# Order of the recurrence branch's output projection: four contraction steps of its second output tile stand ahead of the first tile's last two, and the second tile's weights are split sooner

## The chip, the cores and the metric

One NeuronCore of a Trainium2 chip runs the whole program. The metric is the device time of one execution in microseconds (us); lower is better. Five engines work side by side and meet only at semaphores: PE (TensorE, matrix products; PEld is its weight load), DVE (VectorE), ACT (ScalarE), POOL (GpSimd) and SP (SyncE, which here does nothing but issue transfers, one after another).

## The reference, cut to what matters

The program is a two-layer backbone over 1024 latent tokens and 256 context tokens, 1024 channels wide. The change lies in the first layer, whose output is the sum of two branches behind one projection:

```python
def even_mixer(h, h0, p):
    z = h @ p["w_in"]
    va, vg, ga, xb, gb = jnp.split(z, ...)
    y_a = conformer_conv(va, vg, p) * jax.nn.silu(ga)
    y_b, hT = rglru_branch(xb, p, h0, True)
    y_b = y_b * jax.nn.silu(gb)
    return jnp.concatenate([y_a, y_b], axis=-1) @ p["w_out"], hT
...
x = x + gate[:, None] * out_x
```

The recurrence branch is `y_b`. Its half of the last product, `y_b @ w_out[1024:]`, is 1024 tokens by 1024 channels, contracted over 1024 channels. This product is what the change reorders.

## The kernel before, in words

Everything lies transposed: 128 channels on the partitions, tokens along the free axis, in two halves of 512 (`HALF[0]`, `HALF[1]`). 1024 channels are `KT` = 8 tiles. A product in full precision is made of three rounded ones: a tile is split into a high part (a cast on ACT) and a low part (a subtraction of the cast from the tile), and `hi*hi + hi*lo + lo*hi` is added up in PSUM. So one *contraction step* (one of the eight channel tiles, one half of the tokens) is three matmuls of 128x128 by 128x512, and one output tile of 128 channels is 8 steps x 2 halves x 3 = 48 matmuls.

The part in question comes when the recurrence has ended. The scan's results lie in DRAM (`yb_raw[n]`). For each channel tile n, `gated(n, ...)` (L1040) makes the operand of the projection: per half it loads `yr` (L1044, into one of the two buffers of `vpool`), multiplies it with the gate `sb` (DVE), casts it to `ybh` (ACT), and subtracts to get `ybl` (DVE). Between these, `fill(k)` (L642) puts k pieces of the convolution branch on DVE, which have nothing to do with the projection but have to be done at some time.

While DVE makes those operands, PE computes the gate products `gb4` to `gb7` (48 matmuls each, `gb_product`, L841). Then it goes over to the projection tiles, which the trace calls `wob` (8 output tiles m, two halves each: `wob0_0`, `wob0_1`, `wob1_0` and so on).

Weights come through `gb_weights(j)` (L835): a load into one of two raw buffers (`wr`), a cast into one of two high buffers (`wh`, ACT) and a subtraction into one of two low buffers (`wl`, POOL). Index 4 to 7 is `gb`, 8 to 15 is `wob0` to `wob7`, 16 and 17 are two tiles of the next gate. With two buffers, the raw load of weight j + 2 has to wait for the split of weight j, and the split of j + 2 for the last matmul that uses j.

All of this is issued through `on(engine, ...)` (L497), which chains each instruction behind the one issued before on its engine: the order on PE, ACT, DVE and POOL is the order of the code. Only SP's transfers are placed by the scheduler. Almost all of these instructions are recorded under line L501, so the profile is read by tile names.

The code around the change, with its line numbers:

```python
513    def mm3_fixed(ps, w, xs, cols):
...
516        for k in range(KT):
517            kc = slice(k * P, (k + 1) * P)
518            on("pe", nc.tensor.matmul, ps, hi[:, kc], xh[k][:, cols], start=(k == 0), stop=False)
519            on("pe", nc.tensor.matmul, ps, hi[:, kc], xl[k][:, cols], start=False, stop=False)
520            on("pe", nc.tensor.matmul, ps, lo[:, kc], xh[k][:, cols], start=False, stop=(k == KT - 1))
521            yield
...
532    def raw_split(raw, name):
533        hi = wpool.tile([P, D], F32R, tag="wh", name=f"wh_{name}")
534        lo = wpool.tile([P, D], F32R, tag="wl", name=f"wl_{name}")
535        cast(hi, raw)
536        gp(out=lo, in0=raw, in1=hi.bitcast(F32), op=sub)
537        return hi, lo
...
1040    def gated(n, between):
1041        th, tl = d2tile(f"ybh{n}", F32R), d2tile(f"ybl{n}", F32R)
1042        for h in range(2):
1043            y = vtile(f"yr{n}_{h}")
1044            nc.sync.dma_start(y, yb_raw[n][:, HALF[h]])
1045            vec(nc.vector.tensor_tensor, out=y, in0=y, in1=sbs[n][h], op=mult)
1046            cast(th[:, HALF[h]], y)
1047            fill(1)
1048            vec(nc.vector.tensor_tensor, out=tl[:, HALF[h]], in0=y, in1=th[:, HALF[h]].bitcast(F32), op=sub)
1049            fill(between)
```

In the loop that follows (L1059 to L1069), pass j makes the gate's SiLU `sb` of tile j, then `gated(j - 1)`; in pass 7 the weights of `wob1` are asked for after `gated(6)`. Pass 8 makes `gated(7)`, the last operand. Then the projection begins. Before, its first tile does seven of the eight steps in both halves, and only then the two steps that need the last operand (`ybh7`, `ybl7`). Each finished half is evicted by `wob_evict` (L1072): ACT scales it into `wo`, SP loads the matching piece of x into `xp` (the same two `vpool` buffers that `gated` uses), POOL adds, SP stores to `x1_part`. Behind both evictions of tile m, `gb_weights` splits the weights of tile m + 2. PSUM has four buffers of one bank for these halves (`pm`, L66).

Further on come the layer norm of the convolution branch (its first matmul, `mu`, stands behind `wob5`), the `ga` gate, the projection of the other branch (`woa`), the norm of layer two, and layer two itself (`v`, `g`, `wo`).

Of the kernel before, what the change touches and what calls it, by code (L numbers as in the profile page):

```python
# [20 lines left out]
KT = D // P  # L21
H = 512
HALF = (slice(0, H), slice(H, S))
# [32 lines left out]
def body(ctx, tc, xT, ctxT, cc, ccol, modT, modW, win, gw, wout, wu, grp, wg, wo1, small, edge, ident, outT):  # L56
# [30 lines left out]
    def psum(name):  # L87
        return pm.tile([P, H], F32, tag="mm", name=name)
# [27 lines left out]
    def wload(src, name, eng, n=D, out=None):  # L116
        raw = wpool.tile([P, n], F32, tag="wr", name=f"wr_{name}")
        load(raw, src)
        if out is None:
            hi = wpool.tile([P, n], F32R, tag="wh", name=f"wh_{name}")  # L120
            lo = wpool.tile([P, n], F32R, tag="wl", name=f"wl_{name}")
        else:
            hi, lo = out(f"wh_{name}", F32R), out(f"wl_{name}", F32R)
        split(raw, hi, lo, eng)
        return hi, lo
# [371 lines left out]
    def on(eng, f, *args, **kw):  # L497
        with ExitStack() as octx:
            if eng in last:
                octx.enter_context(tc.issue_after(last[eng].ins))  # L500
            last[eng] = f(*args, **kw)  # L501
        return last[eng]
# [4 lines left out]
    def cast(dst, src):  # L507
        return on("act", nc.scalar.copy, dst, src)
# [4 lines left out]
    def mm3_fixed(ps, w, xs, cols):  # L513
        hi, lo = w
        xh, xl = xs
        for k in range(KT):
            kc = slice(k * P, (k + 1) * P)
            on("pe", nc.tensor.matmul, ps, hi[:, kc], xh[k][:, cols], start=(k == 0), stop=False)
            on("pe", nc.tensor.matmul, ps, hi[:, kc], xl[k][:, cols], start=False, stop=False)
            on("pe", nc.tensor.matmul, ps, lo[:, kc], xh[k][:, cols], start=False, stop=(k == KT - 1))  # L520
            yield

    def all_of(steps):
        for _ in steps:
            pass

    def raw_load(src, name):
        raw = wpool.tile([P, D], F32, tag="wr", name=f"wr_{name}")
        nc.sync.dma_start(raw, src)
        return raw  # L530

    def raw_split(raw, name):
        hi = wpool.tile([P, D], F32R, tag="wh", name=f"wh_{name}")
        lo = wpool.tile([P, D], F32R, tag="wl", name=f"wl_{name}")
        cast(hi, raw)
        gp(out=lo, in0=raw, in1=hi.bitcast(F32), op=sub)
        return hi, lo
# [14 lines left out]
    def vec(f, **kw):  # L552
        return on("vec", f, **kw) if fixed[0] else f(**kw)
# [59 lines left out]
    def ln_sums(by=vadd):  # L613
        for j in range(summed[0], ended[0]):
            for h in range(2):
                first = us[0][:, HALF[h]] if j == 1 else lnacc[h][:, :H]
                by(out=lnacc[h][:, :H], in0=first, in1=us[j][:, HALF[h]], op=add)
        summed[0] = max(summed[0], ended[0])
# [23 lines left out]
    def fill(n):  # L642
        while n > 0:
            try:
                next(going[0])
                n -= 1
            except StopIteration:
                if begun[0] >= whole_[0]:
                    return
                going[0] = conv(begun[0])  # L650
                begun[0] += 1

    with ExitStack() as actx:
# [77 lines left out]
        w = wload(win[3 * KT], "xb0", nc.gpsimd)  # L731
# [5 lines left out]
        w = wload(win[KT], "vg0", nc.gpsimd)  # L737
# [4 lines left out]
        for j in range(KT):  # L742
# [68 lines left out]
            steps = (x for h in range(2) for x in mm3_fixed(xb[:, HALF[h]], wnext, (hh, hl), HALF[h]))  # L811
# [7 lines left out]
            for n, _ in enumerate(gate_steps(j, (gwh, gwl), (uh, ul), gates)):  # L819
# [3 lines left out]
                if n == 9:  # L823
                    w = raw_split(raw, name)
# [7 lines left out]
        gws = {}  # L832


        def gb_weights(j):  # L835
            src, name = ((win[4 * KT + j], f"gb{j}") if j < KT else
                         (wout[j - KT, 1], f"wob{j - KT}") if j < 2 * KT else
                         (win[2 * KT + (0, KT // 2)[j - 2 * KT]], f"ga{(0, KT // 2)[j - 2 * KT]}"))
            gws[j] = raw_split(raw_load(src, name), name)

        def gb_product(j, w):  # L841
            if j == 4:
                gps[j] = (lambda t: [t[:, h] for h in HALF])(wide(f"gb{j}"))
            else:
                gps[j] = [psum(f"gb{j}_{h}") for h in range(2)]
            for h in range(2):
                all_of(mm3_fixed(gps[j][h], w, (hh, hl), HALF[h]))
# [3 lines left out]
        def gb_silu(j):  # L851
            sbs[j] = [ttile(f"sb{j}_{h}") for h in range(2)]
            for h in range(2):
                act(sbs[j][h], gps[j][h], AF.Silu)
# [32 lines left out]
    def d2tile(name, dt=F32):  # L887
        return d2pool.tile([P, S], dt, tag="d2", name=name)
# [5 lines left out]
    def vtile(name):  # L894
        return vpool.tile([P, H], F32, tag="v", name=name)
# [143 lines left out]
    bh, bl = [], []  # L1039
    def gated(n, between):  # L1040
        th, tl = d2tile(f"ybh{n}", F32R), d2tile(f"ybl{n}", F32R)
        for h in range(2):
            y = vtile(f"yr{n}_{h}")
            nc.sync.dma_start(y, yb_raw[n][:, HALF[h]])  # L1044
            vec(nc.vector.tensor_tensor, out=y, in0=y, in1=sbs[n][h], op=mult)
            cast(th[:, HALF[h]], y)
            fill(1)
            vec(nc.vector.tensor_tensor, out=tl[:, HALF[h]], in0=y, in1=th[:, HALF[h]].bitcast(F32), op=sub)
            fill(between)
        bh.append(th)  # L1050
        bl.append(tl)
# [7 lines left out]
    for j in range(3, KT + 1):  # L1059
        if j < KT:  # L1060
            gb_silu(j)
        if 3 < j < KT - 1:
            gb_weights(j + 2)
        if 3 < j < KT - 2:
            gb_product(j + 2, gws[j + 2])
        gated(j - 1, (0, 0, 2, 2, 2, 2, 1, 0)[j - 1])
        if j == KT - 1:
            gb_weights(j + 2)
        ln_sums()  # L1069


# [11 lines left out]
    def ln_mean(h):  # L1083
        lnmu[h], lnsq[h] = banks(f"mu{h}", h)
        on("pe", nc.tensor.matmul, lnmu[h], ones, lnacc[h][:, :H], start=True, stop=True)
# [3 lines left out]
    def ln_square(j, h):  # L1089
        v = us[j][:, HALF[h]]  # L1090
        vec(nc.vector.tensor_tensor, out=v, in0=v, in1=lnmu[h], op=sub)
        if j == 0:
            act(lnsq[h], v, AF.Square)
        else:
            lsq[j, h] = ttile(f"lsq{j}_{h}")
            act(lsq[j, h], v, AF.Square)

    def ln_add(j, h):
        if j > 0:
            vec(nc.vector.tensor_tensor, out=lnacc[h][:, :H] if j == KT - 1 else lnsq[h],  # L1100
                in0=lnsq[h], in1=lsq.pop((j, h)), op=add)
# [3 lines left out]
    def ln_root(h):  # L1105
        ps, lnr[h] = banks(f"ms_ln{h}", h)
        on("pe", nc.tensor.matmul, ps, ones, lnacc[h][:, :H], start=True, stop=True)
        lnrt[h] = ttile(f"sq_ln{h}")
        act(lnrt[h], ps, AF.Sqrt, bias=eps_l)
# [8 lines left out]
        v = us[j][:, HALF[h]]  # L1118
        act(v, v, AF.Silu, bias=col(O_L4 + j), scale=col(O_LNG + j))

    wob_ps = {}
    for m in range(KT):
        w = gws[KT + m]
        wob_ps[m] = [psum(f"wob{m}_{h}") for h in range(2)]
        steps = [mm3_fixed(wob_ps[m][h], w, (bh, bl), HALF[h]) for h in range(2)]
        if m == 0:
            for h in range(2):
                for _ in range(KT - 1):
                    next(steps[h])
        for h in range(2):  # L1130
            all_of(steps[h])
            if m == KT - 2:
                for j in range(KT):
                    ln_square(j, h)
                    if h and j < 2:
                        ln_add(KT - 2 + j, 0)
                    elif j > 1:
                        ln_add(j - 2, h)
            elif m == KT - 1:
                for j in (KT - 2, KT - 1) if h == 0 else ():  # L1140
                    ln_add(j, 1)
                ln_root(h)
            wob_evict(m, h)
            fill(7)
            ln_sums()
        gb_weights(KT + m + 2)
        if m == KT - 3:
            while ended[0] < KT:
                fill(1)
            ln_sums()  # L1150
            for h in range(2):
                ln_mean(h)
# [63 lines left out]
    for i in range(KH):  # L1216
        for j in (i, KH + i) if i else ():
            w = wload(win[2 * KT + j], f"ga{j}", nc.gpsimd)
# [229 lines left out]
    for m in range(0, NK, 2):  # L1448
# [41 lines left out]
        elif m <= KT:  # L1490
            n = 2 * KT + m - 2
# [9 lines left out]
        w = quad(wq, f"g{m}", bx, to_gate, (lambda: wo1_weights(0, 0)) if m == NK - 2 else None)  # L1501
# [30 lines left out]
    for m in range(0, KT, 2):  # L1532
# [30 lines left out]
        w = quad(w, f"wo0_{m}", yops[0], put, nxt)  # L1563
# [10 lines left out]
    for m in range(0, KT - 4, 2):  # L1574
# [14 lines left out]
        w = quad(w, f"wo1_{m}", yops[1], put, ahead)  # L1589
# [118 lines left out]
    m = KT - 4  # L1708
    wa = w
    wb, _, _ = last_half0(m, wa, ahead)  # L1710
# [157 lines left out]
```

## Time and profile before

| | |
|---|---|
| three timed runs | 1301.03, 1304.8, 1307.09 us; median 1304.8 |
| the profiled execution | 1299.17 us, with a span of 1297.4 us from first to last instruction |
| granted TensorE clock, mean | 0.995 |
| PE, busy share by stage | 99.9% in 400 to 500 us; 95.0% in 500 to 540; 100% in 540 to 600; 99.3% in 600 to 700 |
| DVE, busy share by stage | 94.0% in 400 to 500 us; 96.4% in 500 to 540; 77.5% in 540 to 600; 96.5% in 800 to 900 |
| the projection's matmuls | first at 508.8 us, last at 603.3 us |

Times inside the program are microseconds from the span's start. A row of a timeline gives start, duration, engine, line, operation, output <- inputs, and in brackets the idle time of the engine just before and what ended it. A row of the waits gives the engine that waited, the tile it was about to write, what released it, then total, number and longest. Matmuls overlap in their pipeline, so their distance from start to start is the time they cost, not the duration printed. PEclk is the share of full clock that was granted.

### The profile page before, as it was taken

Reading aid. Unit: us, or ns where it says so; the run is one execution under the profiler, and the core shown is the slowest. Engines: PE = TensorE matmul, PEld = TensorE weight load, DVE = VectorE, ACT = ScalarE, POOL = GpSimd, SP = SyncE. Lnnn points to the kernel's source line nnn. Section 1 sums busy time; section 2 is a strip of 40 time slices with the busy share of each in tenths; the row PEclk is TensorE's granted clock in tenths of the full one; section 3 lists DMA queues with packets and bytes.
Section 4 is the critical chain, followed back from the end, with each engine's and each line's share of the span. In section 5 each row is a group of like instructions: output and inputs, shape, how many; then the busy total and the mean of one; then the engine's idle time right before and its main releaser. Section 6 shows DMA issues by size and latency. Waiting matters only on the chain. (4 is left out here: it accounts for less than half of the span.)

```text
span 1297.4 us, 15780 instructions
## 1 busy us (share of the span) xinstructions
PE 1277.9 (98%) x5630; PEld 1026.1 (79%) x5630; DVE 1135.1 (87%) x1758; ACT 632.1 (49%) x921; POOL 353.0 (27%) x180
## 2 busy tenths in 40 slices
PE   9999999999999999999999999999999999999997
PEld 4468888888888887788887888788878788878886
DVE  6979999999999989969789758998999996987876
ACT  4343666566657633227425346734333434654543
POOL 3063655576657612443220032000000000000002
PEclk9999999999999999999999999999999999999998
DMA  9934111121112133443555356244234324778723
GB/s 372 351 123 146 58 41 66 41 74 45 62 41 90 65 106 114 154 146 106 170 177 190 130 183 199 82 155 146 87 133 130 122 93 152 251 242 273 280 80 130
DMA packets 82899, 181.80 MB, mean 140 GB/s; under 512 B 7810, under 2 KB 27650, under 8 KB 82820
## 3 DMA queue, kind: packets, MB, share of 16 engines
q1 hardware_dynamic: 74372, 176.60, 39.6%
q10 hardware_dynamic: 8448, 4.20, 1.1%
q8 instruction: 44, 0.72, 0.2%
q14 instruction: 35, 0.29, 0.1%
HBM read 136.72 MB, written 44.04 MB: 139 GB/s over the span
## 5 line engine op out<-in xcount | busy, mean ns | idle before, releaser
L501 DVE SCALAR_TENSOR_TENSOR conv<-u,sm,conv 128x505 f32<-128x505 f32 (+6 forms) x224 | 153.8, 744 | 0.9
L1669 POOL TENSOR_TENSOR o<-x,rr 128x256 f32<-128x256 f32 (+1 forms) x10 | 9.6, 994 | 444.3 <-ACT rr L1605 444.3
L501 POOL TENSOR_TENSOR l<-l,l 128x1280 f32<-128x1280 f32 (+1 forms) x23 | 64.0, 2797 | 92.0 <-DVE l L501 76.8
L501 ACT ACTIVATE l<-g,sm 128x512 f32<-128x512 f32 (+1 forms) x96 | 58.5, 618 | 57.6 <-PE g L501 57.0
L281 PE MATMUL fold<-graw,wu 128*128 128x512 f32 x128 | 57.3, 608 | 0.0
L501 PE MATMUL wob<-ybh,wh_wob 128*128 128x512 f32 x128 | 51.6, 403 | 1.6 <-ACT ybh L501 1.6
L501 PE MATMUL wob<-ybl,wh_wob 128*128 128x512 f32 x128 | 50.8, 397 | 0.4 <-DVE ybl L501 0.4
L102 ACT CAST wq_g<-wr_g 128x512 fp32r<-128x512 f32 x48 | 28.2, 620 | 47.0 <-DMA wr_g<-wg 14.9
L501 PE MATMUL wob<-ybh,wl_wob 128*128 128x512 f32 x128 | 50.5, 394 | 0.0
L501 PE MATMUL gb<-h0h,wl_gb 128*128 128x512 f32 x128 | 49.9, 390 | 0.1
L501 PE MATMUL vg<-h0h,wl_vg 128*128 128x512 f32 x128 | 50.0, 390 | 0.0
L501 PE MATMUL gb<-h0h,wh_gb 128*128 128x512 f32 x128 | 49.9, 389 | 0.0
L501 PE MATMUL gb<-h0l,wh_gb 128*128 128x512 f32 x128 | 49.8, 389 | 0.0
L501 PE MATMUL vg<-h0l,wh_vg 128*128 128x512 f32 x128 | 49.8, 389 | 0.0
L501 PE MATMUL vg<-h0h,wh_vg 128*128 128x512 f32 x128 | 49.8, 389 | 0.0
L501 PE MATMUL va<-h0h,wh_va 128*128 128x512 f32 x128 | 49.8, 389 | 0.0
L501 PE MATMUL va<-h0l,wh_va 128*128 128x512 f32 x128 | 49.8, 389 | 0.0
L501 PE MATMUL va<-h0h,wl_va 128*128 128x512 f32 x128 | 49.8, 389 | 0.0
L501 DVE TENSOR_TENSOR_SCAN l<-l,l 128x256 f32<-128x256 f32 (+1 forms) x32 | 48.7, 1521 | 1.1
L281 PEld LDWEIGHTS fold<-graw,wu 128*128 128x128 f32 x128 | 25.0, 196 | 30.4 <-issue 29.6
L103 POOL TENSOR_TENSOR wl_wu<-wr_wu,wh_wu 128x1024 fp32r<-128x1024 f32 x8 | 19.3, 2417 | 106.5 <-ACT wh_wu L102 105.7
L501 POOL TENSOR_TENSOR l<-l,uc 128x1280 f32<-128x1280 f32 x16 | 48.1, 3030 | 0.0
(611 smaller groups left out, 4323.4 us busy)
## 6 DMA issues: line engine op xcount, KB each, us to landing
mod<-modT SPq DMA_DIRECT2D x20, 512.0 KB, 5.1
x_part<-xp SPq DMA_DIRECT2D x32, 256.0 KB, 2.5
mod<-modT SPq DMA_DIRECT2D x32, 256.0 KB, 3.0
wr_v<-wfold SPq DMA_DIRECT2D x16, 512.0 KB, 4.2
wr_g<-wg SPq DMA_DIRECT2D x16, 512.0 KB, 4.5
wr_wo<-wo SPq DMA_DIRECT2D x16, 512.0 KB, 4.9
y_b<-y SPq DMA_DIRECT2D x24, 256.0 KB, 3.9
y_t<-y SPq DMA_DIRECT2D x24, 256.0 KB, 4.0
```

Of the source, the lines that this page charges most:

```text
L102: return (nc.scalar.copy(hi, src), eng.tensor_tensor(out=lo, in0=src, in1=hi.bitcast(F32), op=sub))
L103: eng.tensor_tensor(out=lo, in0=src, in1=hi.bitcast(F32), op=sub))
L281: nc.tensor.matmul(ps, w[:, kc], gs[i], start=(i == 0), stop=(i == 3))
L501: last[eng] = f(*args, **kw)
L1669: nc.gpsimd.tensor_tensor(out=outs[k // per][:, k % per], in0=x1[k][:, cols], in1=rr, op=mult)
```

## The change

Two things are done. The request for the weights of `wob1` moves ahead of `gated(6)` in pass 7, so that its cast stands sooner in ACT's order, and its subtraction can run sooner on POOL. And the projection's start is written out: tile 0 does six steps (0 to 5) in both halves, tile 1 does four steps (0 to 3) in both halves, and only then tile 0 does its steps 6 and 7 in the first half, then in the second, each half evicted as it ends; tile 1 goes on with its steps 4 to 7 after that. Tiles 2 to 7 are as before. Nothing is added or removed: 384 matmuls, with the same operands and the same order of summation in each PSUM buffer.

```diff
@@ the loop over the gates (j = 3 .. 8)
             gb_weights(j + 2)
         if 3 < j < KT - 2:
             gb_product(j + 2, gws[j + 2])
-        gated(j - 1, (0, 0, 2, 2, 2, 2, 1, 0)[j - 1])
         if j == KT - 1:
             gb_weights(j + 2)
+        gated(j - 1, (0, 0, 2, 2, 2, 2, 1, 0)[j - 1])
         ln_sums()
@@ the projection
-    wob_ps = {}
+    wob_ps, wob_steps = {}, {}
+
+    def wob_begin(m, n):
+        wob_ps[m] = [psum(f"wob{m}_{h}") for h in range(2)]
+        wob_steps[m] = [mm3_fixed(wob_ps[m][h], gws[KT + m], (bh, bl), HALF[h]) for h in range(2)]
+        for h in range(2):
+            for _ in range(n):
+                next(wob_steps[m][h])
+
+    wob_begin(0, KT - 2)
+    wob_begin(1, 4)
     for m in range(KT):
-        w = gws[KT + m]
-        wob_ps[m] = [psum(f"wob{m}_{h}") for h in range(2)]
-        steps = [mm3_fixed(wob_ps[m][h], w, (bh, bl), HALF[h]) for h in range(2)]
-        if m == 0:
-            for h in range(2):
-                for _ in range(KT - 1):
-                    next(steps[h])
+        if m > 1:
+            wob_begin(m, 0)
         for h in range(2):
-            all_of(steps[h])
+            all_of(wob_steps[m][h])
             if m == KT - 2:
                 for j in range(KT):
                     ln_square(j, h)
```

Three places of the instruction order, before and after. On PE, where tile 0 meets the last operand (a name such as `wob0_1` is tile 0, half 1; `ybh7` is the last operand's high part; the trailing number is a buffer), before:

```order
L501 MATMUL wob0_1_4036<-ybh6_3998,wl_wob0_3971 128x512
L501 MATMUL wob0_0_4035<-ybh7_4021,wh_wob0_3970 128x512
L501 MATMUL wob0_0_4035<-ybl7_4022,wh_wob0_3970 128x512
L501 MATMUL wob0_0_4035<-ybh7_4021,wl_wob0_3971 128x512
L501 MATMUL wob0_1_4036<-ybh7_4021,wh_wob0_3970 128x512
L501 MATMUL wob0_1_4036<-ybl7_4022,wh_wob0_3970 128x512
L501 MATMUL wob0_1_4036<-ybh7_4021,wl_wob0_3971 128x512
L501 MATMUL wob1_0_4122<-ybh0_3690,wh_wob1_4017 128x512
```

And on PE now, from the last matmul of the 24 that tile 1 has ahead:

```order
L501 MATMUL wob1_1_4074<-ybh3_3868,wl_wob1_4001 128x512
L501 MATMUL wob0_0_4035<-ybh6_4004,wh_wob0_3970 128x512
L501 MATMUL wob0_0_4035<-ybl6_4005,wh_wob0_3970 128x512
L501 MATMUL wob0_0_4035<-ybh6_4004,wl_wob0_3971 128x512
L501 MATMUL wob0_0_4035<-ybh7_4021,wh_wob0_3970 128x512
L501 MATMUL wob0_0_4035<-ybl7_4022,wh_wob0_3970 128x512
L501 MATMUL wob0_0_4035<-ybh7_4021,wl_wob0_3971 128x512
L501 MATMUL wob0_1_4036<-ybh6_4004,wh_wob0_3970 128x512
```

The first matmul on `ybh7` stood as the 43rd of the projection and now stands as the 64th; the one on `ybl7` in the second half was the 47th and is the 71st. On ACT, at the SiLU of the last gate, the difference is one cast that moves past two:

```order
 L501 ACTIVATE sb7_1_3995<-gb7_1_3897 128x512
-L501 CAST ybh6_3998<-yr6_0_4000 128x512
-L501 CAST ybh6_3998<-yr6_1_4007 128x512
-L501 CAST wh_wob1_4017<-wr_wob1_4015 128x1024
+L501 CAST wh_wob1_4000<-wr_wob1_3998 128x1024
+L501 CAST ybh6_4004<-yr6_0_4006 128x512
+L501 CAST ybh6_4004<-yr6_1_4013 128x512
```

The weight cast of tile 1 now comes straight behind the gate's SiLU. On SP, the scheduler puts the raw load of tile 3's weights ahead of the last load of `yr`:

```order
 L1044 DMA yr7_0_4023<-yb_raw7_92 128x512
+L529 DMA wr_wob3_4198<-wout 128x1024
 L1044 DMA yr7_1_4029<-yb_raw7_92 128x512
-L529 DMA wr_wob3_4198<-wout 128x1024
```

That load waits for the raw buffer that tile 1's split frees, and what stands behind it on SP waits with it. DVE's and POOL's orders are the same as before from end to end, and so are the other engines' behind this place, but for one store of `x1_part` that passes a load of `xp` on SP.

## The prediction

> **What bounds the kernel now.** I read the page's first part, then the waits of PE over the whole span, then the windows around the projection, then the timelines there.
>
> ```profile
> span 1297.4 us, 15780 instructions
> PE 1277.9 (98%) x5630; PEld 1026.1 (79%) x5630; DVE 1135.1 (87%) x1758; ACT 632.1 (49%) x921; POOL 353.0 (27%) x180
> PE wob L501 <- ACT ybh L501: 1.6, 2, 1.0
> PE qb_v L989 <- DVE vp L1465: 1.4, 2, 0.8
> PE wob L501 <- DVE ybl L501: 0.4, 2, 0.2
> ```
>
> PE is the bound: 98% of the span. Its longest named wait is the projection's for the last operand, `ybh`/`ybl`. "Busy" hides part of it, since the printed durations overlap. So I go to the starts. The timeline of PE at that place:
>
> ```profile
> 508.82 0.39 PE L501 MATMUL wob<-ybh,wh_wob 128*128 128x512 f32 x1
> 509.05 0.39 PE L501 MATMUL wob<-ybl,wh_wob 128*128 128x512 f32 x1
> ...
> 518.35 0.39 PE L501 MATMUL wob<-ybh,wl_wob 128*128 128x512 f32 x1
> 519.78 0.50 PE L501 MATMUL wob<-ybh,wh_wob 128*128 128x512 f32 x1 [1.04 <-ACT ybh L501]
> 520.50 0.50 PE L501 MATMUL wob<-ybl,wh_wob 128*128 128x512 f32 x1 [0.22 <-DVE ybl L501]
> ...
> 522.48 0.50 PE L501 MATMUL wob<-ybl,wh_wob 128*128 128x512 f32 x1 [0.22 <-DVE ybl L501]
> 522.82 0.49 PE L501 MATMUL wob<-ybh,wl_wob 128*128 128x512 f32 x1
> 523.10 0.63 PE L501 MATMUL wob<-ybh,wh_wob 128*128 128x512 f32 x1
> 523.53 0.63 PE L501 MATMUL wob<-ybl,wh_wob 128*128 128x512 f32 x1
> ...
> 526.46 0.39 PE L501 MATMUL wob<-ybh,wl_wob 128*128 128x512 f32 x1
> ...
> 535.58 0.39 PE L501 MATMUL wob<-ybh,wh_wob 128*128 128x512 f32 x1
> ```
>
> Undisturbed, one matmul follows another after 0.227 us (508.82 to 509.05; 42 of them from 508.82 to 518.35). The six that need the last operand come after a gap, and with gaps between them. Then, from 523.10 to 526.46, the distance is 0.43 instead of 0.227. The windows by microsecond (time, PE busy and count, PEclk, DMA) show why:
>
> ```profile
> 522.00:523.00 1.00, 0.78 (x3) 0.99 0.47 170
> 523.00:524.00 1.00, 1.00 (x4) 0.50 0.51 176
> 527.00:528.00 1.00, 1.00 (x6) 1.00 0.76 277
> ```
>
> After the starved stretch the granted clock is 0.50 for some 3.4 us. Of all microseconds before 1287 it is below 0.99 in these only.
>
> **The sum.** Tile 0 and tile 1 are 96 matmuls, from 508.82 to the 97th at 535.58: 26.76 us. At 0.2267 they would be 21.76, so 5.0 are lost, in three pieces.
> - The stall: PE was free at 518.35 + 0.227 = 518.58 and started tile 1 at 523.10. That is 4.52 us for six matmuls worth 6 x 0.2267 = 1.36: 3.16 lost.
> - The half clock: eight matmuls from 523.10 to 526.46 took 3.36 instead of 1.81: 1.55 lost.
> - The remaining 0.3 is a short hitch inside the first 42 and a slow tail; I leave it in.
>
> The change puts tile 1's first 24 matmuls into the hole. What has to hold is that these find their weights, that the last operand is there when it is asked for, and that nothing new comes late behind it. Rows of ACT, POOL, DVE and SP:
>
> ```profile
> 508.58 1.09 ACT L501 ACTIVATE sb<-gb 128x512 f32<-128x512 f32 x2
> 515.00 1.05 ACT L501 CAST wh_wob<-wr_wob 128x1024 fp32r<-128x1024 f32 x1
> 502.54 2.89 POOL L501 TENSOR_TENSOR wl_wob<-wr_wob,wh_wob 128x1024 fp32r<-128x1024 f32 x1 [5.11 <-ACT wh_wob L501]
> 503.86 2.12 DVE L501 TENSOR_TENSOR ybl<-yr,ybh 128x512 fp32r<-128x512 f32 x1
> 511.11 0.68 DVE L501 TENSOR_TENSOR yr<-yr,sb 128x512 f32<-128x512 f32 x1
> 513.20 0.32 SPq L1044 DMA_DIRECT2D yr<-yb_raw  x1
> 515.92 0.32 SPq L1044 DMA_DIRECT2D yr<-yb_raw  x1
> 516.12 2.40 POOL L501 TENSOR_TENSOR wl_wob<-wr_wob,wh_wob 128x1024 fp32r<-128x1024 f32 x1 [10.70 <-ACT wh_wob L501]
> 517.58 1.49 DVE L501 TENSOR_TENSOR yr<-yr,sb 128x512 f32<-128x512 f32 x1 [1.03 <-DMA yr<-yb_raw]
> 521.73 0.69 DVE L501 TENSOR_TENSOR ybl<-yr,ybh 128x512 fp32r<-128x512 f32 x1
> DMA to landing us min/median/max: 2.5/2.6/4.3
> ```
>
> *Weights of tile 1.* The cast goes from 515.00 to right behind the gate's SiLU: 509.67 to 510.72. The two `ybh` casts it passes wait for DVE's `yr` at 511.11 + 0.68, so it delays neither. POOL then subtracts at 510.8 and is done by 513.2 to 513.7 (2.40 to 2.89). PE asks for it after 36 matmuls, at 508.82 + 36 x 0.2267 = 516.98. Cover: 3.3 us.
>
> *A cost on DVE.* While POOL subtracts, a DVE TENSOR_TENSOR does not get through: `ybl` at 503.86 took 2.12 instead of 0.69, ending 0.55 after POOL (502.54 + 2.89 = 505.43), and `yr` at 517.58 took 1.49, also ending 0.55 after POOL's 518.52. So POOL's move from 516.12 to 510.8 frees `yr7`, but hits `yr6` at 511.11: it ends near 513.8 instead of 511.79, 2.0 late. What follows: `ybl6` frees its buffer 2 us later, so the load of `yr7`'s first half goes at 515.2 and lands at 517.8 (2.6) or, like last time, 4.3 later at 519.5; that of the second half goes at 518.0 and lands at 520.6 to 521.5, the raw load of tile 3 being in flight ahead of it. The last `ybl` was done at 521.73 + 0.69 = 522.4; now 522.8 to 523.6. The Trainium skill, SBUF — State Buffer, section "SBUF: two separate sides", says that POOL and a DVE operation with two SBUF inputs lock each other out of a shared port for a whole instruction; both rows agree. By that rule the operand would be late by POOL's whole 2.4 to 2.9 less the 0.3 before `yr6` starts, an estimate that the cover below also holds, so the sum stays.
>
> *The last operand.* PE now asks for it as the 64th to 72nd matmul; the one on `ybl7`'s second half is the 71st, at 508.82 + 70 x 0.2267 = 524.69. Cover: 1.1 to 1.9 us. Without the cover each us late would cost one.
>
> *What is late next.* Tile 2's weights, split behind tile 0's evictions, which now end later while PE reaches tile 2 sooner:
>
> ```profile
> 520.47 2.31 SPq L1076 DMA_DIRECT2D xp<-xT  x2
> 523.40 0.69 ACT L501 ACTIVATE wo<-wob,m 128x512 f32<-128x512 f32 x1 [1.11 <-PE wob L501]
> 523.99 1.03 ACT L501 CAST wh_wob<-wr_wob 128x1024 fp32r<-128x1024 f32 x1
> 525.08 1.28 POOL L501 TENSOR_TENSOR xp<-xp,wo 128x512 f32<-128x512 f32 x1 [0.60 <-DVE conv L501]
> 526.32 2.42 POOL L501 TENSOR_TENSOR wl_wob<-wr_wob,wh_wob 128x1024 fp32r<-128x1024 f32 x1
> ```
>
> Tile 0 ends after 72 matmuls, at 525.1; ACT evicts its second half to 526.0 and casts to 527.0. `xp`'s second load, freed by the last `ybl`, goes at 522.8 to 523.6 and lands 2.6 later (issued at 522.45 above, used at 525.08): 525.5 to 526.2. POOL adds until 527.3 to 527.5 and subtracts until 529.7 to 529.9. PE needs that low part in tile 2's third matmul, whose weights load at about 508.82 + 96 x 0.2267 + 0.25 = 530.8. Cover: 0.9 us, the thinnest place of the change. From tile 3 on, a tile takes 10.9 us of PE and the split behind it under 6.
>
> So PE reaches tile 2 at 530.6 to 530.9 instead of 535.58: 3.16 + 1.55 = 4.7 us sooner.
>
> **Does it reach the end?** The waits of DVE, in 560 to 600 and in 720 to 760 us:
>
> ```profile
> DVE u L501 <- PE mu L501: 11.7, 1, 11.7
> DVE x L1271 <- PE qb_woa L992: 5.7, 3, 2.9
> DVE x L1271 <- PE qc_woa L992: 1.8, 1, 1.8
> ```
>
> DVE has its convolution done 11.7 us before PE comes to the layer norm, so 4.7 less leaves 7.0; at the end of the layer DVE waits for PE again. Layer two starts from there, with the same order on every engine. I take the whole 4.7 and allow 1 for small waits that shift.
>
> Against the profiled execution's own 1299.17 (span 1297.4) that gives 1294.5. The timed runs, 1301.03 to 1307.09, lie 1.9 to 7.9 above it; their mean is 1304.3 and their median 1304.8. I carry the difference to the mean: 1304.3 - 4.7 = 1299.6. About 0.5%, or 6.5 us, is what a measurement of this kernel can tell from no change, so 4.7 (0.36%) counts as no difference.
>
> **The rivals.**
> - *The half clock is not the stall's doing.* Then only 3.16 comes back: 1301.1. For it: the longest gap named there is 1.04 us, and gaps of up to 0.8 us, as at `qb_v` in the first fence, leave the clock alone. Against it: the six starts from 519.78 to 522.82 lie in a stretch of 3.4 us in which 15 fit, the slow stretch follows at once, and no other place has either. The Trainium skill, TensorE: Matmul & The Clock Gate, section "What's actually happening", has the clock halved after an idle window of about 3.4 us, counted in windows that run free of the program; by that rule no gap here is long enough, and the sum would be 3.16. The trace's half clock, 3.4 us long behind a thinned-out stretch, says that a low share is enough.
> - *The gain is given back later.* In 800 to 900 us DVE is busy for 96.48 of 100 and PE for 98.72 (windows by stage, first PE, then its loads, then DVE):
>
> ```profile
> 800.00:900.00 100.00, 98.72 (x434) 80.86 (x433) 96.48 (x170) 54.78 (x95) 0.95 (x8) 1.00 0.36 117
> ```
>
>   If DVE sets the pace there, and the work ahead of it had slack against PE, up to all 4.7 would vanish: 1304.3. Against it: DVE's waits for PE at 580 and in 720 to 760, above.
> - *Slower: the swap on SP.* The last `yr` load now stands behind tile 3's raw load. A raw load took this long to land (KB, us):
>
> ```profile
> wr_wob<-wout SPq DMA_DIRECT2D x1, 512.0 KB, 4.7
> ```
>
>   If the two transfers went one after the other from 518.0, each at its longest (4.7, and 4.3 for `yr`), `yr7` would land at 527.0 and its `ybl`, 2.1 behind (`yr`, a piece of convolution and `ybl`, 0.7 each), end at 529.1. PE would stand 4.4 at the 71st matmul and 0.2 at tile 2, whose split hangs on the same buffer, with a half-clock stretch of 1.55 behind: 6.2 lost, where 4.7 is gained, so 1304.3 + 1.5 = 1305.8. It costs from `ybl7` at 524.4 on, and decides once that ends after 527.8.
> - *The change doesn't do what it says:* out, since the orders of PE, ACT and SP show all of it.
>
> **How the numbers follow.** The forecast (4.7, with 3.7 to 5.7 for shifting waits) 0.62; stall alone 0.14; given back 0.16; slower by the swap 0.05; 0.03 for what I don't see. The timed runs scatter by 3 us to either side, a median of a few by about 2. So the forecast's case shows more than 6.5 about three times in ten: faster 0.19. Slower by 6.5 needs the swap and scatter, or the unseen: 0.03. Same: 0.78. Range: from 1304.3 - 5.7 - 4 = 1294.6 (the execution in the profile lies 5 below the mean, so a fast sample is possible) to 1304.6, which holds stall alone and most of given back.
>
> **What would show it right or wrong.** Right: 0.227 between matmuls from 509 to 536 with no ACT or DVE wait at `wob`; granted clock 1.00 there; the first matmul of `wob2` near 530.7; DVE's wait at `mu` near 7; POOL's `wl_wob` near 510.8 with a DVE `yr` of about 2.7 beside it. Wrong: a wait of PE on `ybl` near 524.7 or on `wl_wob` near 530.8, a half clock that stays, or a `wob2` start at 531 with the span unchanged.

## The result, and the profile after

| | kernel before | changed kernel |
|---|---|---|
| timed runs, median (lowest to highest) | 1304.9 us (1301.03 to 1307.09), 6 runs | 1297.8 us (1293.97 to 1300.15), 6 runs |
| profiled execution | 1299.17 us, span 1297.4 | 1293.97 us, span 1292.2 |

The ratio is 0.995, with a 95% interval of 0.993 to 0.997: the changed kernel is faster by about 7 us, and by 3.9 to 9.1 with the interval. The two profiled executions differ by 5.2. A second comparison (e3 below, 12 runs) gave 0.9964, 0.9948 to 0.9981, or 4.7 us. The forecast was 4.7.

The page of the changed kernel, and its waits of PE over the whole span (engine, line, what it waited for: us in all, times, longest):

```profile
span 1292.2 us, 15780 instructions
PE 1273.8 (99%) x5630; PEld 1025.1 (79%) x5630; DVE 1142.7 (88%) x1758; ACT 632.4 (49%) x921; POOL 353.8 (27%) x180
```
```profile
PE fin_ms L1610 <- DVE dg L1610: 1.3, 1, 1.3
PE ms_n L207 <- DVE dg_n L204: 1.2, 1, 1.2
...
PE qb_v L989 <- DVE vp L1470: 0.7, 2, 0.5
```

The instructions are the same in number. The waits at `wob`, which headed the list before, are gone. A wait in the second layer's norm (`ms_n`, L207) is new. DVE is busy 7.6 us longer (1142.7 against 1135.1); it comes up again below.

The timeline of PE in the projection (start, duration, engine, line, operation). The rows left out all have the same distance:

```profile
508.80 0.39 PE L501 MATMUL wob<-ybh,wh_wob 128*128 128x512 f32 x1
509.03 0.39 PE L501 MATMUL wob<-ybl,wh_wob 128*128 128x512 f32 x1
...
516.96 0.39 PE L501 MATMUL wob<-ybh,wh_wob 128*128 128x512 f32 x1
...
524.67 0.39 PE L501 MATMUL wob<-ybl,wh_wob 128*128 128x512 f32 x1
...
530.56 0.39 PE L501 MATMUL wob<-ybh,wh_wob 128*128 128x512 f32 x1
```

From 508.80 to 530.56 there are 96 matmuls: 21.76 us, which is 96 x 0.2267. The loss there was 5.0 and is 0.0. The windows by microsecond (the number behind POOL's share is the granted clock), at the place where it had read 0.50:

```profile
522.00:523.00 1.00, 1.00 (x6) 0.84 (x5) 1.00 (x3) 0.00 (x0) 0.00 (x0) 1.00 0.16 57
523.00:524.00 1.00, 1.00 (x7) 0.81 (x6) 1.00 (x3) 0.00 (x0) 0.00 (x0) 1.00 0.41 94
```

What hides the moved work, from the timelines of ACT, POOL and DVE of the changed kernel:

```profile
509.57 1.05 ACT L501 CAST wh_wob<-wr_wob 128x1024 fp32r<-128x1024 f32 x1
```
```profile
510.70 2.40 POOL L501 TENSOR_TENSOR wl_wob<-wr_wob,wh_wob 128x1024 fp32r<-128x1024 f32 x1 [5.24 <-ACT wh_wob L501]
...
527.40 2.42 POOL L501 TENSOR_TENSOR wl_wob<-wr_wob,wh_wob 128x1024 fp32r<-128x1024 f32 x1
```
```profile
511.14 2.50 DVE L501 TENSOR_TENSOR yr<-yr,sb 128x512 f32<-128x512 f32 x1
...
521.74 0.69 DVE L501 TENSOR_TENSOR ybl<-yr,ybh 128x512 fp32r<-128x512 f32 x1
```

Tile 1's low weights are there at 513.10, 3.9 us before PE's request at 516.96. Tile 2's are there at 529.82, and PE goes into tile 2 at 530.56 without a gap. Beside POOL's subtraction DVE's `yr` takes 2.50, and ends 0.54 behind POOL. The last `ybl` ends at 522.43, 2.2 ahead of the matmul that reads it (524.67).

How much of that arrives further down, by the same matmul in the profile of before and of after. These are single instructions of the two timelines of PE, first those of before:

```profile
579.10 1.45 PE L501 MATMUL mu<-lnsum,ones 128*128 128x512 f32 x3
...
788.55 1.02 PE L207 MATMUL ms_n<-dg_n,ones 128*128 128x512 f32 x2
...
1238.05 0.39 PE L989 MATMUL qa_l<-y_b11h,wq_wo 128*128 128x512 f32 x1
```
```profile
574.08 1.45 PE L501 MATMUL mu<-lnsum,ones 128*128 128x512 f32 x3
...
785.26 1.12 PE L207 MATMUL ms_n<-dg_n,ones 128*128 128x512 f32 x2 [1.15 <-DVE dg_n L204]
...
1232.81 0.39 PE L989 MATMUL qa_l<-y_b11h,wq_wo 128*128 128x512 f32 x1
```

PE is 5.0 ahead at the layer norm, 3.3 behind the new wait in the second layer's norm, and 5.2 near the end. In this pair of executions the wait gave back 1.7, and other waits later regained it.

### The profile page after: what moved, and what is told of

It reads as the page before. It is cut to its first block, busy times and chain, and to the rows that moved or that the text cites. A ratio compares the mean times of both kernels' runs of the same rounds, so it can differ in the third digit from the quotient of the medians.

```text
span 1292.2 us, 15780 instructions
## 1 busy us (share of the span) xinstructions
PE 1273.8 (99%) x5630; PEld 1025.1 (79%) x5630; DVE 1142.7 (88%) x1758; ACT 632.4 (49%) x921; POOL 353.8 (27%) x180
```

## The experiments

The theory: PE stood because the last operand came late; four steps of tile 1 fill that time if their weights are split by then, and the half clock goes with the stall. The rivals: the half clock has another cause; one part of the change does all; the gain is given back downstream. All ratios are to the kernel before on the same chip: 1302.5 us in the median of 35 runs beside e1 to e4, 1302.6 of 35 beside e5 to e8.

**e1: only the weights are split sooner.** The order of PE stays that of before.

```diff
-        gated(j - 1, (0, 0, 2, 2, 2, 2, 1, 0)[j - 1])
         if j == KT - 1:
             gb_weights(j + 2)
+        gated(j - 1, (0, 0, 2, 2, 2, 2, 1, 0)[j - 1])
```

> Only the sooner split of tile 1's weights; PE's order as before. Theory (the gain is the hole in PE's row at 518.6 to 523.1 us and the half clock behind it): no gain, within 1.5 us of the kernel before; POOL's subtraction runs near 510.7 instead of 516.1, a DVE multiplication of yr beside it takes about 2.5 us instead of 0.7, the last operand is ready at 522.4 as before, and PE's hole and half clock stay as they were. Rival (the sooner split is worth something by itself, since it takes POOL out of the way of the last yr): the last operand comes sooner by 1 us or more, and the time falls by 1 to 3 us.

Measured: 1304.8, ratio 1.0017 (1.0001 to 1.0033): slower by 2.2 us (0.1 to 4.3). PE's timeline has the gap of before and a new one ahead of it; DVE's shows where both come from:

```profile
514.35 0.50 PE L501 MATMUL wob<-ybh,wh_wob 128*128 128x512 f32 x1 [1.29 <-ACT ybh L501]
...
521.06 0.50 PE L501 MATMUL wob<-ybh,wh_wob 128*128 128x512 f32 x1 [0.43 <-ACT ybh L501]
...
535.23 0.39 PE L501 MATMUL wob<-ybh,wh_wob 128*128 128x512 f32 x1
```
```profile
511.14 2.51 DVE L501 TENSOR_TENSOR yr<-yr,sb 128x512 f32<-128x512 f32 x1
...
519.66 0.69 DVE L501 TENSOR_TENSOR yr<-yr,sb 128x512 f32<-128x512 f32 x1 [1.27 <-DMA yr<-yb_raw]
...
523.01 0.69 DVE L501 TENSOR_TENSOR ybl<-yr,ybh 128x512 fp32r<-128x512 f32 x1
```

The sooner split alone does harm, where the expectation had the hole unchanged and no change over 1.5 us: `yr6` is held up by POOL as it is in the changed kernel, so PE, which without the moved steps comes to `ybh6` in its seventh step, waits 1.3 there, and `yr7` comes later (the last `ybl` ends at 523.70, in before at 522.42). From the first `wob` to tile 2, 4.65 is lost. Of that nothing is half clock, which stays away from the projection in this execution. Before's loss without its half clock was 3.45, so the split alone adds 1.2 to the stall. The other 1.0 may be the clock's in the other executions. Each run lists its mean granted clock: over the 12 of e1 it is 0.9943, over the 35 of before 0.9951 (standard errors 0.0003 and 0.0002). One half-clock stretch of 3.41 us takes 0.5 x 3.41 / 1303 = 0.0013 off the mean, so e1 has 0.6 such stretches more per execution, give or take 0.3, at 1.55 each.

**e2: only the order of steps.** The diff's `wob_begin` part; the split stays where it was.

> Only the new order of the steps on PE; tile 1's weights are split behind gated(6) as before. Theory: PE asks for tile 1's weights at 516.98 and gets the low part at 518.5, so a new wait of about 1.1 to 1.3 us on wl_wob appears near 517.4; the hole at the last operand is gone, with the half clock; 4.7 - 1.2 = 3.5 us gained. Rival (the split is what matters): less than 1.5 us gained. Rival (the low share of matmuls halves the clock even at 1.2 us): a half-clock stretch follows and about 2 us are gained.

Measured: 1300.3, ratio 0.9977 (0.9961 to 0.9993): faster by 3.0 us (0.9 to 5.1). PE has one stop left (the first row; the second is POOL's):

```profile
519.04 0.50 PE L501 MATMUL wob<-ybh,wl_wob 128*128 128x512 f32 x1 [0.93 <-POOL wl_wob L501]
```
```profile
516.62 2.37 POOL L501 TENSOR_TENSOR wl_wob<-wr_wob,wh_wob 128x1024 fp32r<-128x1024 f32 x1 [10.68 <-ACT wh_wob L501]
```

It is the first product with tile 1's low weights, which POOL has ready at 516.62 + 2.37 = 518.99. The loss is 1.22 instead of 5.0, and there is no half clock (mean over the 12 runs 0.9963, 0.0012 above before). So the steps bring most, and the sooner split takes out the last 1.2. The parts don't add up on their own: +2.2 and -3.0 make -0.8, together they make -4.7. The cost of the split lies on an operand that PE asks for early in e1 and late in the changed kernel.

**e3 and e4: the changed kernel and the kernel before, again**, beside the runs of the kernel before, to see how much is scatter. No edit.

> The changed kernel once more, in five rounds. The three-round comparison gave 7 us between the means, the profiles 5.2. Theory (the hole alone, 4.7 to 5.0): the ratio comes out near 0.996, 4 to 6 us, and the excess over 5 was scatter. Rival (there is more than the hole that one profile shows): 7 us or more again.

> The kernel before against itself, with a second profile. It gives the scatter of the comparison (ratio 1.000, within 1.5 us) and a second look at the hole. Theory: again 3 to 3.5 us of waits at the last operand and a half clock of about 3.4 us behind them, 4.5 to 5.2 us in all. Rival (the half clock depends on where its window happens to lie): another loss, the clock at 1.00 behind the hole or a second half-clock stretch elsewhere.

Measured: e3 1298.1, ratio 0.9964 (0.9948 to 0.9981), 4.7 us faster (2.5 to 6.8). e4 1303.8, ratio 1.0009 (0.9994 to 1.0024): no difference. In e4's profile the hole and the half clock are back, 4.51 lost; its windows:

```profile
521.00:522.00 1.00, 0.48 (x2) 0.29 (x1) 0.98 (x2) 1.00 (x2) 0.00 (x0) 0.65 0.52 176
522.00:523.00 1.00, 1.00 (x3) 0.64 (x3) 1.00 (x3) 0.08 (x1) 0.00 (x0) 0.50 0.34 127
...
792.00:793.00 1.00, 1.00 (x4) 0.81 (x3) 0.77 (x2) 0.51 (x2) 1.00 (x1) 0.50 0.63 258
...
921.00:922.00 1.00, 1.00 (x4) 0.80 (x3) 1.00 (x3) 0.00 (x0) 0.00 (x0) 0.50 0.00 0
```

In e3 nothing is lost in the projection either (0.0). But both profiles have two more half-clock stretches, near 790 and 920, each behind one wait. PE's waits, e3 first and then e4:

```profile
PE qb_v L989 <- DVE vp L1470: 2.5, 1, 2.5
PE ms_n L207 <- DVE dg_n L204: 2.0, 1, 2.0
```
```profile
PE ms_n L207 <- DVE dg_n L204: 2.7, 1, 2.7
PE qb_v L989 <- DVE vp L1465: 2.5, 1, 2.5
```

These two waits come and go from one execution to the next in both kernels. Set beside the first profile of the same kernel matmul by matmul, e4 falls 4.5 us behind at the first place and 3.5 at the second, e3 2.5 and 3.9. That is most of why e3's profiled execution took 1301.83 and e4's 1306.43, while the first profiles took 1293.97 and 1299.17: two single executions differ by 7 to 8 us without any change. Pair by pair the difference is 4.6 and 5.2.

**e5: the kernel before, with its hole filled by useless work.** Twelve matmuls on operands that have long been there stand between the first 42 and the last six. Their sums go into a PSUM tile that tile 1 then overwrites; they are work that the reference doesn't need.

```diff
+            idle = psum("wob1_0")
+            for k in range(12):
+                kc = slice((k % 4) * P, (k % 4 + 1) * P)
+                on("pe", nc.tensor.matmul, idle, w[0][:, kc], bh[k % 4][:, HALF[0]], start=True, stop=True)
+            wob_ps[1] = [idle, psum("wob1_1")]
```

> The kernel before, with twelve more matmuls of the same size placed in PE's row between tile 0's seventh steps and its last ones; their result is overwritten, so they are work that nobody needs. They fill 12 x 0.227 = 2.7 us of the hole, whose end is set by the last operand at 522.4. Theory (the half clock is the doing of the thin stretch): clock 1.00 throughout, tile 1 starts at 523.1 as before, and the 1.55 us of the half clock come back: 1.5 us faster than before, tile 2 at about 534. Rival (the half clock has another cause): clock 0.50 for 3.4 us behind 523 all the same, and no gain or a loss of up to 0.3 us.

Measured: 1298.2, ratio 0.9979 (0.9963 to 0.9996): faster by 2.7 us (0.5 to 4.8) with twelve matmuls more. PE's timeline and windows:

```profile
518.05 3.11 PE L501 MATMUL wob<-ybh,wh_wob 128*128 128x512 f32 x13
...
533.43 0.39 PE L501 MATMUL wob<-ybh,wh_wob 128*128 128x512 f32 x1
```
```profile
522.00:523.00 1.00, 1.00 (x5) 0.82 (x6) 1.00 (x2) 0.61 (x2) 0.19 (x1) 1.00 0.20 53
523.00:524.00 1.00, 1.00 (x6) 0.84 (x5) 1.00 (x3) 1.00 (x2) 1.00 (x1) 1.00 0.84 225
```

The clock stays at 1.00. From the first `wob` (508.29) to tile 2 it is 25.13 us, against 26.76 and 26.27 in the two profiles of before: 1.1 to 1.6 sooner, about the 1.55 that was put down to the half clock. PE does nothing more that is useful here, and the operand comes no sooner; only the thin stretch is gone. So the half clock goes with the thin stretch. This one profile would not show it alone, since e1's has a stall without a half clock behind it. The time of the twelve runs agrees with it, and so does the count of thin steps in the last section; the mean clock of the runs (0.9958 against 0.9953, which is 0.4 of a stretch, give or take 0.3) agrees less firmly.

**e6, e7 and e8: one, two and six steps of tile 1 ahead** instead of four.

```diff
-    wob_begin(1, 4)
+    wob_begin(1, 1)    (e6; 2 in e7, 6 in e8)
```

> The changed kernel with one step of tile 1 ahead instead of four. Theory: PE waits 1.9 us in pieces for the last operand (the 43rd to the 54th matmul start between 518.3 and 522.7 instead of evenly), nine of the 15 matmuls that fit start in the last 3.4 us. With the clock untouched 2.9 us of the 4.7 stay; if a share of nine in 15 is low enough to halve the clock, 1.4 us stay. Rival (the order of the steps doesn't matter, the sooner split does): as fast as with four.

> The changed kernel with two steps of tile 1 ahead instead of four. Theory: one wait of about 0.5 us at the last operand's second half (needed at 521.9, ready at 522.4), clock 1.00; 4.2 of 4.7 us stay, the same as with four within the scatter. Rival (the cover has to be four steps): a loss of over 1.5 us against four.

> The changed kernel with six steps of tile 1 ahead instead of four, all for which the operand is there. Tile 0 then ends 2.7 us later while PE reaches tile 2 at the same 530.6. Theory (the thinnest cover is 0.9 us, at tile 2's low weights): tile 2's split ends at about 532.5, PE waits for it for 1.5 to 2 us near 531, and 3 us of the 4.7 stay. Rival (tile 2's weights have more room than the prediction gives them): no wait there, as fast as with four.

| steps ahead | lost from first `wob` into tile 2 | ratio (95%) | against before |
|---|---|---|---|
| 1 (e6) | 2.05 us | 0.9988 (0.9969 to 1.0007) | -1.6 (-4.0 to +0.9) |
| 2 (e7) | 1.18 | 0.9983 (0.9968 to 0.9998) | -2.2 (-4.2 to -0.3) |
| 6 (e8) | 1.6 | 0.9994 (0.9978 to 1.0011) | -0.8 (-2.9 to +1.4) |

The stops of PE, by its timelines in e7 and in e8, and POOL's split of tile 2's weights in e8:

```profile
522.11 0.51 PE L501 MATMUL wob<-ybh,wh_wob 128*128 128x512 f32 x1 [0.37 <-ACT ybh L501]
522.84 0.50 PE L501 MATMUL wob<-ybl,wh_wob 128*128 128x512 f32 x1 [0.22 <-DVE ybl L501]
```
```profile
532.47 0.50 PE L501 MATMUL wob<-ybh,wl_wob 128*128 128x512 f32 x1 [1.40 <-POOL wl_wob L501]
```
```profile
530.02 2.40 POOL L501 TENSOR_TENSOR wl_wob<-wr_wob,wh_wob 128x1024 fp32r<-128x1024 f32 x1
```

With too few steps ahead PE still comes early to the last operand. With one ahead the clock stays at 1.00 there: the two steps of 3.41 us with the stops have 0.67 and 0.73 of work, counted as in the last section, and that is not low enough to halve it. Two is nearly enough, but the wait comes twice, where one of 0.5 us was expected: for `ybh` and then for the `ybl` that DVE makes from it, each about 0.5 us longer than a matmul. A part of it is that DVE waited 0.5 for the last `yr` in this execution. With six ahead tile 0 ends later, and with it its eviction, which tile 2's split stands behind; POOL is done at 532.42 and PE stops for 1.6, as expected. Four lies between: no stop on either side. The projection's ranking (4 best, 2, 6, 1) is that of one trace each, two for four steps. The times agree with it in that all three gain less than e3, but their intervals overlap, e3 ran on another chip, and one step ahead comes out before six. The time gained is 1.1 to 2.3 less than the projection's gain (4.7 less the loss) in each of the three; e7's and e8's profiles have a half-clock stretch at 789 behind the norm's wait, e6's one at 917. Whether that is the same scatter or a systematic return is not settled by 10 runs.

## Why the prediction was right, point by point

- *The stall goes (3.16), with or without the 0.3 of small gaps.* The stall went, and the small gaps with it: tile 2 began at 530.56 (forecast 530.6 to 530.9), and of the 5.0 nothing is left.
- *The half clock goes with the stall (1.55).* It did, and e5 takes it away by filling the stall alone. But the stall doesn't always bring it. e1 lost 4.65 to gaps at a clock of 1.00. How often, the runs' mean clocks tell: 0.9951 and 0.9953 for the kernel before (35 runs each), 0.9962 for the changed one (12 runs, standard error 0.0003). The 0.0010 between them is 0.8 of a stretch of 0.0013, give or take 0.3, if the other places are the same in both. So on average, by this estimate, the half clock is worth 0.8 x 1.55 = 1.2, and with the 3.45 of gaps the projection gives back 4.7: what e3 measured. That the forecast has the same 4.7 is in part luck: it left out the 0.3 of small gaps and counted 0.3 too much for the half clock. The Trainium skill, TensorE: Matmul & The Clock Gate, section "What's actually happening", asks for an idle window of about 3.4 us; here matmuls ran in the window before each half clock, and PE stood for no longer than 1.42 - 0.23 = 1.2 us at a time in before (518.35 to 519.78). The measurement decides: a low share is enough.
- *Tile 1's weights, cover 3.3.* POOL was done at 513.10, cover 3.9. e2 shows what it costs if the split isn't moved: 1.2.
- *POOL holds up `yr6`.* 2.50 us, ending at 513.64 (forecast 2.7 and 513.8). e1 shows that this cost is real where nothing hides it.
- *The last operand at 522.8 to 523.6.* 522.43 in the changed kernel's profile, 0.4 sooner than forecast, 522.73 + 0.69 = 523.4 in e3's, 523.70 in e1. In e1 the first half's load of `yr7` landed late, one of the prediction's two cases; in e3 it was the second half's (below). The cover was 2.2 in the first profile and 1.6 in e3's (the 71st matmul starts at 525.05 there); it was needed in both.
- *Tile 2's weights at 529.7 to 529.9, the thinnest place.* 529.82, no stop. e8 moved this place and stopped there, so it is a bound for how many steps can go ahead.
- *DVE's wait at `mu` of 7.0.* This step failed. DVE waited 2.4:

```profile
DVE u L501 <- PE mu L501: 2.4, 1, 2.4
```

  Before, DVE began to wait at 580.16 - 11.70 = 568.46; now at 575.14 - 2.42 = 572.72, 4.3 later. I had moved PE's arrival by 4.7 and left DVE's as it was. But POOL's work came sooner too (tile 1's split by 5.4, tile 3's by 3.5, those from tile 4 on by 5.0), and met other operations of DVE. The groups of DVE in 505 to 580 us (count, busy, mean ns of one), before and after:

```profile
L501 DVE TENSOR_TENSOR yr<-yr,sb 128x512 f32<-128x512 f32 x5 | 4.2, 845 | 1.0 <-DMA yr<-yb_raw 1.0
L501 DVE TENSOR_TENSOR lnsum<-lnsum,u 128x512 f32<-128x512 f32 x4 | 3.0, 789 | 0.0
...
L501 DVE TENSOR_TENSOR u<-u 128x512 f32<-128x512 f32 x2 | 1.4, 694 | 0.1
```
```profile
L501 DVE TENSOR_TENSOR yr<-yr,sb 128x512 f32<-128x512 f32 x5 | 5.2, 1050 | 0.0
L501 DVE TENSOR_TENSOR lnsum<-lnsum,u 128x512 f32<-128x512 f32 x4 | 4.3, 1112 | 0.0
...
L501 DVE TENSOR_TENSOR u<-u 128x512 f32<-128x512 f32 x2 | 3.5, 1761 | 0.1
```

  The same instructions take 1.0, 1.3 and 2.1 more, and `edge_junk` 0.9 (two, from 160 to 584 ns): 5.3, less the 1.0 for which DVE no longer waits on `yr`. It cost nothing, since 2.4 us of cover were left; with 4 us less of slack from the start, DVE would have set the pace here, and 4.0 - 2.4 = 1.6 of the gain would have been lost.
- *Given back later* (rival, to 1304.3): not as a whole, since the times have 4.7 (2.5 to 6.8) in e3. In the first pair 1.7 was given back at `ms_n` and regained; in e3 and e4 both kernels wait there. All six traces with steps of tile 1 ahead have this wait, of 1.2 to 3.5 us, and two of the four without (e1 and e4, 2.0 and 2.7). Whether the sooner arrival makes it more likely is open.
- *Slower by the swap on SP* (rival): in the first profile the last `yr` load, issued at 517.76 behind the raw load of tile 3, landed in time, and the last `ybl` was not late. In e3 it was issued at 518.12, and DVE stood for it:

```profile
521.35 0.69 DVE L501 TENSOR_TENSOR yr<-yr,sb 128x512 f32<-128x512 f32 x1 [0.62 <-DMA yr<-yb_raw]
...
522.73 0.69 DVE L501 TENSOR_TENSOR ybl<-yr,ybh 128x512 fp32r<-128x512 f32 x1
```

  In e7 and e8 it stood 0.5 and 0.2 there, and in no trace without the swap. So the swap may cost a little on the operand, but the end of 529.1 that the rival priced did not come, and with four steps ahead the cover held.
- *The time.* 1299.6 forecast, 1297.8 and, in e3, 1298.1 measured. The kernel before took 1302.5 beside e3, so there the forecast's 4.7 would be 1297.8. The first comparison, 0.55%, is just past the 0.5% that I took for the limit of what can be told, the second, 0.36%, inside it; "no change at all" lies outside either interval. The excess of the first over 4.7 did not repeat in the second, which fits the scatter that the prediction allowed for.

## What to carry to other kernels

An operand that comes late on a bound engine can be covered by work of the next tile, and fully if that tile's own weights come sooner too (without, 1.2 of the 5.0 was left); count how many steps the next tile can lend before its end delays the one after (here four of eight, since two leave a stop and six make another; three and five were not tried). Work that moves in time meets other work: the operations of POOL that came up to 5.4 us sooner met other operations of DVE, which cost 4.3 us and were hidden with 2.4 to spare. And before a difference of half a per cent is explained, the kernel before should be measured against itself, with its profiles compared: here two waits that come and go make 6 to 8 us between single executions.

## What the runs showed of the hardware that was not expected

- *The half clock comes on a grid.* Each stretch lasts 3.41 us, and the three of e4 begin at 521.30, 790.95 and 920.66, the two of e3 at 786.72 and 916.42: 79, 38 and 38 steps of 3.413 us. From the starts of PE's matmuls I worked out for each step of 3.41 us, at the projection and near 916, the share in which PE worked, one matmul counted for 0.2267 us at most. Six steps with 0.18 to 0.39 (three to six matmuls, where fifteen fit) were followed by a half clock; four with 0.41 (e1), 0.42 (e8), 0.43 (e2) and 0.46 (e1) were not, and none with more. So it hangs on how the gaps fall on the grid, which is another in each execution: a loss of this size brings it (before, e4) or not (e1). This is worked out from ten places, not tried on purpose; those near 790 are left out, since the matmuls of `ms_n` there cost more than the others.
- *Where an execution's time scatters.* ACT waits for the weights' transfer `wr_g` 3.5 us at the longest in the first profile of before and 3.1 in that of after, but 5.4 in e4 and 5.8 in e3, the same ones in which PE stands 2.5 us at `qb_v`:

```profile
ACT wq_g L102 <- DMA wr_g<-wg: 6.0, 2, 3.5
```
```profile
ACT wq_g L102 <- DMA wr_g<-wg: 7.9, 2, 5.8
```

  (The first is the kernel before in its first profile, the second e3, both in 770 to 925 us.) All ten traces have this order: where the longest wait for `wr_g` is 2.8 to 3.5, PE stands 0.2 to 0.6 for DVE at `qb_v`; with 3.8 to 4.6 it is 1.8 or 1.9, with 5.4 and 5.8 it is 2.5. That the transfer is the cause was not tried; the waits go together.
- *A small instruction can be held too.* `edge_junk`, 128x8 with a sum beside it, took 1.00 us instead of 0.16 beside POOL's addition into `xp`, while the larger SCALAR_TENSOR_TENSORs of the convolution kept their 0.74 on average (742 and 743 ns over 31 of them). In the kernel these add to a sum that lies in PSUM, so only one of their two tiles is in SBUF, while `edge_junk` reads two there; whether that makes the difference was not tried:

```profile
553.72 1.00 DVE L501 SCALAR_TENSOR_TENSOR edge_junk<-u,sm 128x8 f32<-128x8 f32 x1
...
554.77 2.83 DVE L501 TENSOR_TENSOR u<-u 128x512 f32<-128x512 f32 x1
```
